# Input projections of a hybrid decoder block in seven quarter products, in two passes over the tokens

## The chip, the cores and the metric

The kernel runs on one core of a Trainium2 chip. Its time is the device time of one execution in microseconds (us). The core has engines that run side by side, each through its own list of instructions in order: PE (matmuls; PEld is its loading of weights), DVE and POOL (elementwise work), ACT (functions and copies), and SP, which issues the DMAs. POOL can't read PSUM, the memory into which PE writes. The order on each engine is fixed when the program is built: a planner places every instruction by the order of the source and by its own estimate of when its operands are there. At run time an instruction that is not ready holds up everything behind it on its engine.

## What is computed

A decoder block over 2048 tokens of width 1024, all in float32:

```python
xn = rmsnorm(h, pre_gain[i])
z = xn @ w_in[i]
q, k, v, fl, g_attn, x_lru, g_lru = jnp.split(z, SPLIT_POINTS, axis=-1)
...
y_attn = rmsnorm(o_attn, attn_out_gain[i]) * jax.nn.silu(g_attn)
xc = causal_depthwise_conv(x_lru, conv_w[i], conv_b[i])
o_lru = rg_lru(xc, ...)
y_lru = rmsnorm(o_lru, lru_out_gain[i]) * jax.nn.silu(g_lru)
mix = jnp.concatenate([y_attn, y_lru], axis=-1) @ w_out[i]
h = h + rmsnorm(mix, post_gain[i])
...
```

`w_in` has 6152 columns: six groups of 1024 (queries, keys, values, gate of the attention, input and gate of the recurrence) and 8 forget logits. `o_attn` is causal attention of 8 heads of 128 whose scores get a bias from the cumulated forget logits; `o_lru` a gated linear recurrence over the tokens. A second matmul with a gate and per-layer embeddings follows; the change doesn't touch it.

## The kernel before

Every float32 operand of a matmul is split in two parts, a high one (ACT copies it to the type that PE reads, line 46) and a low one, the difference (DVE or POOL, line 52). `mm3` then makes three matmuls of a product: high-high, high-low, low-high (lines 60 to 62).

**Projections.** All tokens of `x`, times the gain of the norm, lie in SBUF in both parts (`xh`, `xl`: four chunks of 512 tokens, lines 230 to 234). Beside it the sum of squares of every token is made (line 244), and its root is applied to the results (`rx`, `rs_x`), so matmuls don't wait for it. Values come first: four groups of 256 columns, tokens on partitions, the last group with the forget logits as well (264 columns, `project_v`). Then for each of 8 blocks of 128 features (loop at line 342): the input of the recurrence with its convolution, its gate, the keys, then the recurrence itself (lines 385 to 421), and queries and attention gate of the block before. `load_w` loads a block of weights (two loads of 512 columns' worth) and splits it, with POOL making the lows; `project` makes 24 matmuls of 128x512 for each chunk of 512 tokens: 8 pieces of the contraction times 3. Keys, queries, values and gates go to DRAM as float32 (`kT_d`, `qT_d`, `v_d`, `gT_d`).

**Attention.** 8 heads times 4 groups of 512 queries. While one group's scores are made, the values of the group before are (`merge`). `scores` takes 512 keys at a time; DVE adds the bias and keeps the row's extreme (line 553), ACT makes the exponential (560). `values` transposes the weights on PE (582), splits them (`th` on ACT, `tl` on DVE) and multiplies them with the values. The inverse of the row sums makes a round trip through DRAM (`r_d` out at line 565, `rb` back at 567) and is applied at line 594. The next head's keys and values come in eight pieces during the head before (`load_part`): each is loaded into a buffer `kvf` (two of them), copied by ACT into `kh` or `vh` (line 451 or 455) and completed by POOL (`kl`, `vl`); queries likewise (`split_q`), with the low on DVE. POOL also adds the causal mask to pieces of bias that come by DMA (`dg`, lines 490 and 491). The first head's pieces and queries are loaded beside the last projections (lines 499 to 504). In the last head the weights of the output projection are loaded through `kvf` too.

The order of the blocks and `tc.high_priority` at two places are by hand; the rest is the planner's. A tile's pool has a number of buffers (`bufs`); a new tile waits until its buffer is free.

## Time and profile before

| | us |
|---|---|
| median of three runs (2438.3 to 2449.4) | 2444.1 |
| the profiled execution, first to last instruction (span) | 2421.5 |
| projections, by PE's timeline | 5.5 to 1139.1 |
| attention, seven heads of eight (1150 to 1730) | 580 |

The span is that of one profiled execution, and its total device time is not on the page; the runs of the table were other executions. An engine's "busy" time counts the instructions that it runs. Matmuls overlap in PE's pipeline, so the time of one is read from how many run in a stretch, not from its own duration. In rows of groups the columns are line, engine, operation, output and inputs, shape and count, then busy us and mean ns of one, then idle time before them with what ended it.

### The profile page before, as it was taken

The page shows a single profiled execution, that of the slowest core. Times are in us where ns is not written, and L with a number is a line of the kernel's source. Part 1 is how long each engine was busy: PE and PEld are TensorE (multiplying, and loading weights), DVE is VectorE, ACT ScalarE, POOL GpSimd, SP SyncE. Part 2 cuts the span into 40 slices and gives each one's busy share as a digit, 9 for nine tenths or more (in the row PEclk, how much of TensorE's full clock was granted, in tenths as well). Part 3 has the DMA queues.
Part 4 walks back from the last instruction along what each step waited for, and adds up shares of the span by engine and source line. Part 5 has one row for each costly group of instructions (what it writes and reads, how often), then busy time and mean ns, then how long its engine had stood idle before and what let it go on. Part 6 is the DMA issues. An engine that isn't in the chain of part 4 may idle for free.

```text
span 2421.5 us, 30623 instructions
## 1 busy us (share of the span) xinstructions
PE 2288.7 (95%) x11297; PEld 1895.9 (78%) x11297; DVE 1208.3 (50%) x2193; ACT 908.0 (37%) x1526; POOL 665.1 (27%) x594
## 2 busy tenths in 40 slices
PE   8999999999999999999778778988789999999999
PEld 8998888888888888887667667766668787788887
DVE  5222764555554646363666666766552413433333
ACT  7311432324241414232545545655452423211111
POOL 0210422324141314131322333233242322322221
PEclk9999999999999999999899889999899999999999
DMA  9411111112121212125555555455443635433332
GB/s 327 131 49 31 63 59 57 63 53 70 46 76 40 76 48 74 44 74 138 157 128 124 115 130 140 124 140 131 113 127 109 226 119 191 130 121 110 113 101 83
DMA packets 190519, 257.50 MB, mean 106 GB/s; under 512 B 31648, under 2 KB 104608, under 8 KB 190368
## 3 DMA queue, kind: packets, MB, share of 16 engines
q1 hardware_dynamic: 190224, 255.49, 35.4%
q8 instruction: 89, 1.46, 0.3%
q14 instruction: 62, 0.51, 0.1%
q10 hardware_dynamic: 144, 0.05, 0.0%
HBM read 179.65 MB, written 75.83 MB: 106 GB/s over the span
## 4 chain that ended last, share of the span: by engine, by line
PE 33%; DMA 11%; DVE 3%; issue 2%; ACT 2%; POOL 1%; SPq 0%; DVEq 0%; ACTq 0%; POOLq 0%
PE bank L60 7%; PE bank L62 7%; PE bank L61 7%; DMA kvf<-kT_d 4%; PE tbank L582 3%; DMA dg<-nb_d 2%; PE obank L60 2%; DMA kvf<-in_w_o_dram 2%; PE obank L61 2%; PE obank L62 2%; DMA kvf<-v_d 1%; DMA r_d<-r 1%; DMA ya_d<-gs 1%; DVE pr L553 1%; PE sbank L62 1%
## 5 line engine op out<-in xcount | busy, mean ns | idle before, releaser
L60 PE MATMUL bank<-xh,wh 128*128 128x512 f32 x1280 | 506.0, 395 | 0.0
L61 PE MATMUL bank<-xl,wh 128*128 128x512 f32 x1280 | 505.9, 395 | 0.0
L62 PE MATMUL bank<-xh,wl 128*128 128x512 f32 x1280 | 505.9, 395 | 0.0
L61 PEld LDWEIGHTS bank<-xl,wh 128*128 128x128 f32 x1280 | 240.5, 188 | 58.1
L62 PEld LDWEIGHTS bank<-xh,wl 128*128 128x128 f32 x1280 | 240.5, 188 | 58.0
L60 PEld LDWEIGHTS bank<-xh,wh 128*128 128x128 f32 x1280 | 240.5, 188 | 57.7
L52 DVE TENSOR_TENSOR tl<-tbank,th 128x512 fp32r<-128x512 f32 (+1 forms) x320 | 191.0, 607 | 165.9 <-ACT th L46 164.5
L582 PE MATMUL tbank<-ident,pr 128*128 128x128 f32 x1088 | 182.3, 285 | 43.1 <-DVE tl L52 42.0
L46 ACT ACTIVATE th<-tbank 128x512 fp32r<-128x512 f32 (+1 forms) x320 | 164.3, 527 | 93.5 <-PE tbank L582 89.3
L582 PEld LDWEIGHTS tbank<-ident,pr 128*128 128x128 f32 x1088 | 138.7, 147 | 75.3 <-DVE tl L52 44.8
L60 PE MATMUL obank<-th,vh 128*128 128x512 f32 (+1 forms) x320 | 129.4, 404 | 62.5 <-ACT th L46 58.5
L491 POOL TENSOR_TENSOR dg<-dg,cmask 128x128 f32<-128x128 f32 x128 | 60.8, 478 | 424.5 <-DMA dg<-nb_d 313.8
L52 POOL TENSOR_TENSOR wl<-wf,wh 128x512 fp32r<-128x512 f32 x70 | 96.0, 1393 | 265.1 <-ACT wh L46 265.1
L560 ACT ACTIVATE pr<-pr,m 128x128 f32<-128x128 f32 (+15 forms) x128 | 153.1, 1197 | 11.5 <-DVE m L553 11.5
L60 PE MATMUL bank<-wvh,xh 128*128 128x256 f32 (+1 forms) x512 | 144.2, 285 | 7.2 <-ACT wvh L46 7.2
L52 POOL TENSOR_TENSOR yo<-yf,yh 128x1024 fp32r<-128x1024 f32 x32 | 76.9, 2403 | 254.1 <-ACT yh L46 245.0
L62 PE MATMUL bank<-wvh,xl 128*128 128x256 f32 (+1 forms) x512 | 144.7, 284 | 0.0
L61 PE MATMUL bank<-wvl,xh 128*128 128x256 f32 (+1 forms) x512 | 144.3, 283 | 0.0
L61 PE MATMUL obank<-tl,vh 128*128 128x512 f32 (+1 forms) x320 | 138.4, 432 | 1.1 <-DVE tl L52 1.1
L60 PE MATMUL sbank<-kh,qh 128*128 128x512 f32 (+3 forms) x320 | 127.6, 399 | 9.8 <-DVE m L553 8.8
L60 PEld LDWEIGHTS obank<-th,vh 128*128 128x128 f32 x320 | 64.3, 201 | 85.6 <-ACT th L46 69.1
L61 PE MATMUL sbank<-kl,qh 128*128 128x512 f32 (+3 forms) x320 | 121.4, 379 | 0.0
(214 smaller groups left out, 4668.8 us busy)
## 6 DMA issues: line engine op xcount, KB each, us to landing
wf<-in_w_t_dram SPq DMA_DIRECT2D x80, 256.0 KB, 2.9
xr<-in_x_dram SPq DMA_DIRECT2D x16, 512.0 KB, 6.6
v_d<-vo SPq DMA_DIRECT2D x64, 128.0 KB, 2.1
kT_d<-st SPq DMA_DIRECT2D x32, 256.0 KB, 2.1
yl_d<-G SPq DMA_DIRECT2D x32, 256.0 KB, 2.1
qT_d<-st SPq DMA_DIRECT2D x32, 256.0 KB, 2.1
gT_d<-st SPq DMA_DIRECT2D x32, 256.0 KB, 2.2
dg<-nb_d SPq DMA_DIRECT2D x32, 256.0 KB, 5.7
```

Source lines behind the costliest of these rows:

```text
L46: nc.scalar.activation(hi, src, AF.Copy)
L52: eng.tensor_tensor(out=lo, in0=src, in1=f32(hi), op=ALU.subtract)
L60: nc.tensor.matmul(out, lhsT=wh, rhs=xh, start=start, stop=False)
L61: nc.tensor.matmul(out, lhsT=wh, rhs=xl, start=False, stop=False)
L62: nc.tensor.matmul(out, lhsT=wl, rhs=xh, start=False, stop=stop)
L491: nc.gpsimd.tensor_tensor(out=dg[:, n - P:n], in0=dg[:, n - P:n], in1=cmask, op=ALU.add)
L553: nc.vector.tensor_tensor_reduce(out=pr[:, a:z], in0=b[:, :z - a], in1=dg if z == L else u.bias[:, a:z], scale=-1.0, scalar=BIG if m is No ...
L560: nc.scalar.activation(pr[:, :L], pr[:, :L], AF.Exp, bias=m, scale=-1.0, accum_out=r4[:, i:i + 1])
L582: nc.tensor.transpose(b[:, i * P:(i + 1) * P], u.P[i][:, sb * P:(sb + 1) * P], ident)
```

## The change

The projections are grouped into products of two halves by two halves: the contraction (1024) in two halves, two blocks of features, and two chunks of 512 tokens. Instead of the eight products of quarters, seven products of sums of quarters are made, with Strassen's and Winograd's formulas. `operands` makes the seven sums of the weights: six loads of 512 columns, four sums on DVE, seven splits on ACT and POOL. `x_sums` makes those of `x`. `combine` runs the seven products (`by_feature`: 12 matmuls of 512 columns each; `by_token` for values: 24 of 256), adds later products onto banks of earlier ones where the formula allows it, and makes the remaining sums on DVE (five for each combination, with two copies on ACT).

The seven operands of `x` for 1024 tokens fill the room of the old `xh` and `xl`, so the tokens go in two passes. Weights are loaded and split in each pass. The operands of the second pass are made during the first (`x_sums(2, ...)`, in four of its blocks), written to `bx_d` and read back between the passes. `x` is scaled by its root mean square before the split (`stats`, `x_piece`), so results need no scaling any more. The forget logits get matmuls of their own (`project_forget`). In a pass, each block makes the recurrence's input and gate as one combination, keys and queries as one, and every second block the gates of two heads as one.

Keys, queries and values are stored as high and low part (`two_parts`), and attention loads both parts straight into the operands' tiles; `kvf`, its copies and its differences go for them. The first head's loads stand behind the projections. The queries' factor moves into the constant of the instruction at line 553 and that of the bias. The recurrence keeps its formulas, with its temporary tiles in one set of six buffers.

```diff
-    kT_d = dram.tile([NH, P, S], F32, name="kT_d")
+    kT_d = dram.tile([2, NH, P, S], F32, name="kT_d")
...
+    ORDER = (1, 6, 5, 7, 2, 3, 4)
...
+    def parts(src, el, hi=None, lo=None):
+        if hi is None:
+            hi = wk.tile([P, 512], F32R, name="wh", bufs=NWH)
+            lo = wk.tile([P, 512], F32R, name="wl", bufs=NWH)
+        split(nc, src, hi, lo, "act", el)
+        return hi, lo
+    def operands(load, nq):
+        def raw(r, q):
+            t = wk.tile([P, 512], F32, name="wf", bufs=NWF)
+            src = load(r, q)
+            nc.sync.dma_start(out=t.rearrange("p (a b) -> p a b", b=src.shape[-1]), in_=src)
+            return t
+        def tt(out, a, b, op):
+            nc.vector.tensor_tensor(out=out, in0=a, in1=b, op=op)
+            return out
+        qs = range(nq)
+        yield 1, [parts(raw(11, q), "pool") for q in qs]
+        s1, s2, s3 = [], [], []
+        for q in qs:
+            a21, a22, a11 = raw(21, q), raw(22, q), raw(11, q)
+            s1.append(tt(a22, a21, a22, ALU.add))
+            s3.append(tt(a21, a11, a21, ALU.subtract))
+            s2.append(tt(a11, s1[q], a11, ALU.subtract))
+        yield 6, [parts(s2[q], "pool") for q in qs]
+        yield 5, [parts(s1[q], "pool") for q in qs]
+        yield 7, [parts(s3[q], "pool") for q in qs]
+        a12 = [raw(12, q) for q in qs]
+        yield 2, [parts(a12[q], "pool") for q in qs]
+        yield 3, [parts(tt(s2[q], a12[q], s2[q], ALU.subtract), "pool") for q in qs]
+        yield 4, [parts(raw(22, q), "pool") for q in qs]
+    def combine(load, nq, units, product, sinks):
+        B = [{} for _ in units]
+        for num, ws in operands(load, nq):
+            for n, u in enumerate(units):
+                t = B[n]
+                if num in (1, 5, 6, 7):
+                    t[num] = bank()
+                    product(t[num], num, ws, u, True)
+                else:
+                    product(t[{2: 1, 3: 5, 4: 7}[num]], num, ws, u, False)
+                if num == 1 or num == 5:
+                    t["p", num] = ev()
+                    nc.scalar.activation(t["p", num], t[num], AF.Copy)
+                elif num == 6:
+                    t["u"] = t["p", 1]
+                    nc.vector.tensor_tensor(out=t["u"], in0=t[6], in1=t["p", 1], op=ALU.add)
+                elif num == 7:
+                    t["v"] = t["p", 5]
+                    nc.vector.tensor_tensor(out=t["p", 5], in0=t["p", 5], in1=t["u"], op=ALU.add)
+                    c22, done = sinks(u, 22)
+                    nc.vector.tensor_tensor(out=c22, in0=t[7], in1=t["p", 5], op=ALU.add)
+                    done(c22)
+                elif num == 2:
+                    sinks(u, 11)(t[1])
+                else:
+                    c, done = sinks(u, 12 if num == 3 else 21)
+                    nc.vector.tensor_tensor(out=c, in0=t[5 if num == 3 else 7], in1=t["u"], op=ALU.add)
+                    done(c)
+    bs_ = {}
...
+    def by_feature(out, num, ws, u, start):
+        (wh, wl), = ws
+        wh, wl = (w.rearrange("p (k f) -> p k f", f=P) for w in (wh, wl))
+        bh, bl = bs_[num]
+        for k in range(4):
+            for n, (w, x_) in enumerate(((wh, bh), (wh, bl), (wl, bh))):
+                nc.tensor.matmul(out, lhsT=w[:, k], rhs=x_[:, k], start=start and k == 0 and n == 0,
+                                 stop=k == 3 and n == 2, skip_group_check=True)
+    def by_token(out, num, ws, u, start):
+        bh, bl = bs_[num]
+        for i in range(2):
+            ts = slice((2 * u + i) * P, (2 * u + i + 1) * P)
+            for k in range(4):
+                wh, wl = (w.rearrange("p (k f) -> p k f", f=256)[:, k % 2] for w in ws[k // 2])
+                for n, (x_, w) in enumerate(((bh, wh), (bh, wl), (bl, wh))):
+                    nc.tensor.matmul(out[:, i * 256:(i + 1) * 256], lhsT=x_[:, k, ts], rhs=w,
+                                     start=start and i == 0 and k == 0 and n == 0,
+                                     stop=i == 1 and k == 3 and n == 2, skip_group_check=True)
+    def halves(i1, i2):
+        return lambda r, q: w_t[i1 if r < 20 else i2, :, (r % 10 - 1) * 4:(r % 10) * 4]
+    def two_parts(src, store, el="pool"):
+        hi, lo = evr("sh"), evr("sl")
+        split(nc, src, hi, lo, "act", el)
+        for i, part in enumerate((hi, lo)):
+            store(i, f32(part))
...
+    def stats(t0, pool):
+        ss = wk.tile([P, 8], F32, name="ss", bufs=2)
+        for i in range(4):
+            for j in range(2):
+                xr = pool.tile([P, 512], F32, name="xt")
+                nc.sync.dma_start(out=xr, in_=x[(t0 + i) * P:(t0 + i + 1) * P, j * 512:(j + 1) * 512])
+                nc.scalar.activation(xr, xr, AF.Square, accum_out=ss[:, j * 4 + i:j * 4 + i + 1])
+        s4 = wk.tile([P, 4], F32, name="s4", bufs=2)
+        nc.vector.tensor_tensor(out=s4, in0=ss[:, 0:4], in1=ss[:, 4:8], op=ALU.add)
+        rsqrt_small(rs_x[:, t0:t0 + 4], s4, wk, 4)
+        b = bank()
+        for i in range(4):
+            dg = pool.tile([P, P], F32, name="dg0", bufs=2)
+            nc.vector.tensor_scalar(dg, ident, rs_x[:, t0 + i:t0 + i + 1], None, ALU.mult)
+            nc.tensor.matmul(b[:, i * P:(i + 1) * P], lhsT=onesq, rhs=dg, start=True, stop=True)
+        rx = pool.tile([P, 512], F32, name="rx", bufs=2)
+        nc.scalar.activation(rx, b, AF.Copy)
+        return rx
...
+    def x_piece(c, k, rx, pool):
+        t = pool.tile([P, 512], F32, name="xt")
+        nc.sync.dma_start(out=t, in_=xT[c, :, k])
+        nc.vector.scalar_tensor_tensor(out=t, in0=t, scalar=vec[:, PRE + k:PRE + k + 1], in1=rx,
+                                       op0=ALU.mult, op1=ALU.mult)
+        return t
+    def x_sums(c, k, rxs, pool):
+        def sub(out, a, b):
+            nc.vector.tensor_tensor(out=out, in0=a, in1=b, op=ALU.subtract)
+            return out
+        b11 = x_piece(c, k, rxs[0], pool)
+        yield 1, b11
+        b12 = x_piece(c + 1, k, rxs[1], pool)
+        t1 = sub(b11, b12, b11)
+        yield 5, t1
+        b22 = x_piece(c + 1, k + 4, rxs[1], pool)
+        yield 7, sub(b12, b22, b12)
+        yield 3, b22
+        t2 = sub(b22, b22, t1)
+        yield 6, t2
+        b21 = x_piece(c, k + 4, rxs[0], pool)
+        yield 2, b21
+        yield 4, sub(b21, b21, t2)
...
+    def project_forget(p):
+        lhs = []
+        for j in range(2):
+            w = wk.tile([P, 4, P], F32R, name="wff", tag="wh", bufs=NWH)
+            nc.gpsimd.memset(f32(w), 0.0)
+            f = wk.tile([P, 4, 8], F32, name="wf8", bufs=2)
+            nc.sync.dma_start(out=f, in_=w_f[:, 4 * j:4 * j + 4])
+            split(nc, f, w[:, :, 0:8], w[:, :, 8:16], "act", "dve")
+            lhs.append(w)
+        for i, use in enumerate((((1, 0), (2, 1)), ((1, 0), (5, 0), (3, 1)))):
+            b = bank()
+            n, last = 0, len(use) * 8 - 1
+            for num, j in use:
+                for k in range(4):
+                    for part in bs_[num]:
+                        nc.tensor.matmul(b, lhsT=lhs[j][:, k], rhs=part[:, k], start=n == 0, stop=n == last)
+                        n += 1
+            z = ev()
+            nc.vector.tensor_copy(z[:16], b[:16])
+            nc.sync.dma_start(out=zf_d[:, (2 * p + i) * 512:(2 * p + i + 1) * 512], in_=z[:16])
...
+    def project_kq(p, hb):
+        def sinks(u, c):
+            dst = qT_d if c > 20 else kT_d
+            cs = slice((2 * p + c % 10 - 1) * 512, (2 * p + c % 10) * 512)
+            def store(i, part):
+                nc.sync.dma_start(out=dst[i, hb, :, cs], in_=part)
+            if c == 11:
+                return lambda b: two_parts(b, store, "dve")
+            return ev(), lambda z: two_parts(z, store)
+        combine(halves(5 * hb + 2, 5 * hb + 3), 1, range(1), by_feature, sinks)
...
+            pe = pool_(p0, "pe", NXT0, side="right")
+            rxs = [stats(0, pe), stats(4, pe)]
+            gens = [x_sums(0, k, rxs, pe) for k in range(4)]
+            for i in range(1, 8):
+                bs_[i] = new_b(i)
+            for _ in range(7):
+                for k in range(4):
+                    i, t = next(gens[k])
+                    parts(t, "dve", bs_[i][0][:, k], bs_[i][1][:, k])
...
+                if i == 1 and p == 0:
+                    nc.vector.tensor_copy(halo[:, hb], X[:, 512:515])
+            def gate(i):
+                sg = lt()
+                nc.scalar.activation(sg, Gs[i], AF.Sigmoid)
+                nc.vector.tensor_tensor(out=Gs[i], in0=Gs[i], in1=sg, op=ALU.mult)
+            def sinks(u, c):
+                i = c % 10 - 1
+                if c == 11:
+                    def take(b):
+                        nc.scalar.activation(Xs[0][:, 3:], b, AF.Copy)
+                        conv(0)
+                    return take
+                if c == 12:
+                    return Xs[1][:, 3:], lambda z: conv(1)
+                return Gs[i], lambda z: gate(i)
+            combine(halves(5 * hb, 5 * hb + 1), 1, range(1), by_feature, sinks)
+            for i in range(2):
+                XC, G = XCs[i], Gs[i]
+                XH, XL = lt(F32R, "XH"), lt(F32R, "XL")
+                split(nc, XC, XH, XL, "act", "pool")
+                R, I, Dn = lt(), lt(), lt()
+                for gi, (dst, bias) in enumerate(((R, BR), (I, BI))):
+                    b = bank()
+                    mm3(nc, b, (wgh[:, gi], wgl[:, gi]), (XH, XL), True, True)
+                    nc.scalar.activation(dst, b, AF.Sigmoid, bias=vec[:, bias + hb:bias + hb + 1])
...
+        for p in range(2):
+            if p == 1:
+                for i in ORDER:
+                    bs_[i] = new_b(i)
+                    for n in range(2):
+                        nc.sync.dma_start(out=f32(bs_[i][n]), in_=bx_d[i - 1, n])
+            project_forget(p)
+            for j in range(2):
+                project_v(p, j)
+            if p == 0:
+                rxs = [stats(8, xq), stats(12, xq)]
+            else:
+                xq_stack.close()
+                forget(pool_(pl_, "cw"))
+            for hb in range(NH):
+                recurrent(p, hb)
+                project_kq(p, hb)
+                if hb % 2:
+                    project_ga(p, hb - 1)
+                if p == 0 and 1 <= hb < 5:
+                    k = hb - 1
+                    for i, t in x_sums(2, k, rxs, xq):
+                        for n, part in enumerate(parts(t, "pool")):
+                            nc.sync.dma_start(out=bx_d[i - 1, n, :, k], in_=f32(part))
+            sl = wk.tile([P, 8], F32, name="sl", bufs=1)
+            channel_sums(sl, accl, 0, 8, bank)
+            rsqrt_small(rstd_l[:, 8 * p:8 * p + 8], sl, wk, 8)
+    p1.close()
+    ps1.close()
...
-        f = ap.tile([P, 4, P], F32, name="kvf", bufs=2) if h else wp.tile([P, 4, P], F32, name="wf")
-        if n % 2 == 0:
-            cs = slice(c * 512, (c + 1) * 512)
-            f = f.rearrange("p a b -> p (a b)")
-            nc.sync.dma_start(out=f, in_=kT_d[h, :, cs])
-            split(nc, f, s.kh[:, cs], s.kl[:, cs], "act", "pool" if h else "dve")
-        else:
-            bs = slice(c * 4, c * 4 + 4)
-            nc.sync.dma_start(out=f, in_=v_d[h, :, bs])
-            split(nc, f, s.vh[:, bs], s.vl[:, bs], "act", "pool" if h else "dve")
...
+        for i in range(2):
+            if n % 2 == 0:
+                nc.sync.dma_start(out=f32((s.kh, s.kl)[i][:, cs]), in_=kT_d[i, h, :, cs])
+            else:
+                nc.sync.dma_start(out=f32((s.vh, s.vl)[i][:, bs]), in_=v_d[i, h, :, bs])
...
-        u.qh, u.ql = early_q.pop(g) if h == 0 and g in early_q else split_q(h, g)
+        for i, q in enumerate((u.qh, u.ql)):
+            nc.sync.dma_start(out=f32(q), in_=qT_d[i, h, :, g * 512:(g + 1) * 512])
...
-                                               scale=-1.0, scalar=BIG if m is None else m,
+                                               scale=-QSCALE, scalar=BIG if m is None else m,
```

403 lines of the change are left out of this document (126 added, 277 removed).

## The prediction

> **What bounds the kernel now.** I read the page's totals first, then busy time by stretches, then PE's timeline at the seams, and last who waited for whom inside attention.
>
> ```profile
> span 2421.5 us, 30623 instructions
> PE 2288.7 (95%) x11297; PEld 1895.9 (78%) x11297; DVE 1208.3 (50%) x2193; ACT 908.0 (37%) x1526; POOL 665.1 (27%) x594
> ...
> 0.00:30.00 30.00, 22.85 (x168) 22.30 (x169) 20.09 (x47) 23.08 (x43) 2.74 (x13) 1.00 0.97 345
> 5.40:1139.10 1133.70, 1131.95 (x5625) 948.77 (x5626) 565.40 (x810) 381.95 (x565) 293.43 (x221) 1.00 0.23 78
> 120.00:180.00 60.00, 60.00 (x509) 60.00 (x508) 12.14 (x56) 9.97 (x21) 12.67 (x5) 1.00 0.18 49
> 500.00:600.00 100.00, 100.00 (x431) 80.64 (x430) 49.76 (x65) 30.48 (x42) 27.44 (x21) 1.00 0.17 55
> 1150.00:1730.00 580.00, 488.17 (x2646) 406.83 (x2646) 389.10 (x967) 322.65 (x598) 182.34 (x223) 0.91 0.53 130
> ...
> 1139.14 0.22 PE L60 MATMUL sbank<-kh,qh 128*128 128x128 f32 x1
> ...
> L46 ACT ACTIVATE kh<-kvf 128x512 fp32r<-128x512 f32 x28 | 17.7, 631 | 121.5 <-DMA kvf<-kT_d 120.7 <-POOL dg L491 0.8
> ```
>
> The rows of stretches give window, length, busy time of PE, PEld, DVE, ACT and POOL, PE's clock, the DMA share and GB/s. The projections last until 1139 us (the last row but one, the first score). From 5.4 us on PE never stops in them: 431 matmuls of 512 columns in 100 us are **0.232 us** each, 509 of 256 columns (V) in 60 us are **0.118 us**. DVE is half busy there, POOL a quarter. Attention is another matter: PE is idle for 92 of 580 us and its granted clock is 0.91. Those 580 us hold the loads of 28 pieces of keys (last row), four a head, so seven heads, and a head takes 83 us. The runs shown have a median of 2444.1, 22.6 over this span; I take these 22.6 as unchanged, so that a difference in the span is a difference in the time.
>
> **The change, part by part.**
>
> *Matmuls.* A pair of feature blocks over all tokens needs 2 x 4 x 24 = 192 matmuls now; two passes of seven products of 12 need 168. Twenty pairs: 3360 for 3840, so 480 x 0.232 = 111 us less. V: 1344 for 1536, 192 x 0.118 = 23 us less. The forget logits leave V's last group (8 of 264 columns, 1 us) and become 80 matmuls of their own, 19 us more. PE's work falls by about **116 us**. The Trainium skill, TensorE: Matmul & The Clock Gate, section "Back-to-back issue gap", gives about 131 ns for each 512-column matmul in a stream; at that figure the 480 would be worth 63 us, but the 0.232 above was measured in this kernel, and it decides.
>
> *What the seven products ask of the other engines.* Take one cycle: two head blocks in one pass, with two recurrent, two key/query and one gate combination.
>
> ```profile
> L402 DVE RECIPROCAL Dn<-Dn 128x512 f32<-128x512 f32 x32 | 107.3, 3354 | 1.1
> L406 DVE TENSOR_TENSOR X<-X,Dn 128x512 f32<-128x512 f32 x32 | 22.5, 704 | 0.4
> L409 DVE TENSOR_TENSOR_SCAN R<-Dn,carry,I 128x512 f32<-128x512 f32 x24 | 31.7, 1323 | 1.0
> L233 DVE SCALAR_TENSOR_TENSOR xl<-xf,vec,xh 128x512 fp32r<-128x512 f32 x24 | 16.6, 747 | 4.7 <-ACT xh L232 4.7
> L408 DVE TENSOR_SCALAR Dn<-Dn 128x512 f32<-128x512 f32 x20 | 8.4, 419 | 0.0
> L420 POOL TENSOR_TENSOR R<-R 128x512 f32<-128x512 f32 x28 | 29.2, 1041 | 64.0 <-DVE G L413 64.0
> L46 ACT ACTIVATE wh<-wf 128x512 fp32r<-128x512 f32 x80 | 46.2, 623 | 100.3 <-PE bank L61 93.6 <-DMA wf<-in_w_t_dram 6.7
> ...
> 694.71 1.29 POOL L52 TENSOR_TENSOR wl<-wf,wh 128x512 fp32r<-128x512 f32 x1 [1.26 <-ACT wh L46]
> 695.96 1.74 POOL L52 TENSOR_TENSOR wl<-wf,wh 128x512 fp32r<-128x512 f32 x1
> ...
> 695.32 0.63 DVE L334 SCALAR_TENSOR_TENSOR st<-bank,rx 128x512 f32<-128x512 f32 x1
> 695.87 0.69 DVE L406 TENSOR_TENSOR X<-X,Dn 128x512 f32<-128x512 f32 x1
> 696.66 1.60 DVE L407 TENSOR_TENSOR I<-I,X 128x512 f32<-128x512 f32 x1
> ```
>
> PE: 5 x 84 + 24 for the gates = 444 matmuls, **103 us**. DVE: each combination makes 4 sums of weights and 5 sums of results (45), the two recurrent blocks 12 more two-tensor operations, the key/query lows 2: 59 x 0.69 = 41. 20 of the scalar-and-two-tensors kind x 0.75 = 15, 8 x 0.42, 4 reciprocals x 3.35 = 13, 4 scans x 1.3 = 5, small copies 1: **79 us**. POOL: 35 lows of weights, 6 of results, 12 in the recurrence: 53 x 1.29 + 4 x 1.04 + two small ones = **75 us**. ACT: 35 + 10 + 12 copies of 0.62 and the recurrence's functions, some 67 us, which stays beside PE. So each by itself fits under PE's 103.
>
> But DVE and POOL are not by themselves. In the last five rows POOL's second `wl` starts at 695.96 while DVE's L406 runs, and takes 1.74 where the first took 1.29; DVE's L407 starts within it, and ends at 698.26, 0.56 after POOL's end: 1.60 where L406, of the same form, took 0.69. Each **waited for the other to finish**. L334, which reads PSUM and one tile of SBUF, ran beside POOL in 0.63: such operations don't take part. Where now 27 of 100 us are POOL's, meetings are rare; after the change POOL fills 75 of 103. The Trainium skill, GPSIMD Engine Reference, section "Specifications", says that POOL's SBUF interfaces are shared with VectorE and names contention with instructions of two SBUF inputs or in a 2-port mode; it gives no price, and the 1.60 agrees.
>
> The price of a meeting lies between 0 (as L334) and 0.91 (1.60 - 0.69). In a cycle 68 DVE operations have two SBUF inputs or are of the fast 0.42 kind (5 for each combination, 25 in all; convolution 12; gates, tail of the recurrence and silu 31). Half of them follow another one directly (three in a convolution, five in the recurrence's tail, three sums of weights); POOL takes its turn between those, so they pay 0.91, and the first of a run about half. With POOL busy for 0.72 of the time: 0.72 x (34 x 0.91 + 34 x 0.45) = 33 us. DVE then needs 79 + 33 = **112 us a cycle**, over PE's 103: the projections go at DVE's pace. Ends: 103 (no cost, PE rules) and 79 + 0.72 x 68 x 0.91 = 123.
>
> *Eight cycles.* 896 us. In pass 0 four blocks also make the sums of the later tokens: 4 x (4 x 0.75 + 4 x 0.69 + 8 x 0.72 x 0.68) = 39 us of DVE. So pass 0 takes 487, pass 1 448.
>
> *Start.* Now the first matmul runs at 5.5 us and PE loses 7 us in the first 30 (row above). Afterwards x is scaled by its rms, so 4.2 MB of statistics come before it: 12 us at the 345 GB/s of that row, and squares, root and broadcast bring the first piece to about 18 us. DVE then owes 16 pieces x 0.75 + 16 differences x 0.69 + 28 lows x 0.69 = 42 us; the last operand is ready at 60. Until then PE can run four products of V's first group (192 x 0.118 = 23) and the forget logits (9): 28 us idle. V and logits of a pass are 672 x 0.118 + 9 = 89 us, so this part ends at 117.
>
> *Seam of the passes.* 14.7 MB of operands come back, 43 us at 345 GB/s, each pair as soon as its last product is done; the rest of the last combination (17 us) and V's products (5.7 us each against 6.1 us of loading) cover all but some 5 us. Bounds: nothing, and 43 - 17 = 26. I take 5.
>
> *End of the projections.*
>
> ```profile
> rb<-r_d SPq DMA_DIRECT2D x32, 256.0 KB, 4.4
> ...
> kvf<-kT_d SPq DMA_DIRECT2D x28, 256.0 KB, 4.7
> ```
>
> The first head's keys and queries came in beside the last projections; now their tiles take the place of the recurrence's and are loaded after it. No row shows it; two loads of 4.7 us one after the other (the last number is the median from issue to landing) make 9, and 0 is the other end; I take 8, as nothing else is ready then.
>
> Projections: 117 + 487 + 5 + 89 + 448 + 8 = **1154**, against 1139: +15.
>
> *Attention.* Splitting of keys, values and queries goes.
>
> ```profile
> 1241.23 0.46 POOL L491 TENSOR_TENSOR dg<-dg,cmask 128x128 f32<-128x128 f32 x1 [13.82 <-DMA dg<-nb_d]
> ...
> 1242.09 1.23 SPq L565 DMA_DIRECT2D r_d<-r  x1
> ...
> 1253.20 0.32 SPq L567 DMA_DIRECT2D rb<-r_d  x1
> ...
> 1249.60 0.63 ACT L46 ACTIVATE kh<-kvf 128x512 fp32r<-128x512 f32 x1 [11.94 <-DMA kvf<-kT_d]
> ...
> 1250.74 0.69 DVE L52 TENSOR_TENSOR tl<-tbank,th 128x512 fp32r<-128x512 f32 x1 [10.05 <-ACT th L46]
> ...
> 1251.49 1.11 PE L582 MATMUL tbank<-ident,pr 128*128 128x128 f32 x4 [8.59 <-DVE tl L52]
> ...
> PE obank L60 <- ACT th L46: 58.5, 23, 14.9
> PE tbank L582 <- DVE tl L52: 42.0, 11, 9.4
> ...
>   DMA kvf<-kT_d: 120.7, 27
>   DMA kvf<-v_d: 40.8, 16
> ```
>
> Read upwards from PE: it stood 8.59 us for DVE's `tl`, which stood 10.05 for ACT's `th`, which was queued behind `kh`, which stood 11.94 for the load of the **next** head's keys; that load needed a buffer that POOL frees, and POOL stood 13.82 for a bias. ACT lost 162 us so. With the parts loaded straight into their tiles, a head ahead, nothing of this is left on ACT or POOL (POOL's lows moved to the projections, and are in the 75 above). What PE loses now is 92 us idle and 0.09 x 580 = 52 at the lowered clock; the gain lies between 0 and 144. Next in line is the round trip of 1/sum: `r_d` goes out at 1242.09, SP can issue `rb` only at 1253.20, and it lands 4.4 us later, 15 us in all. After a head's first group PE has only some 8 us of work (128 x 10 columns of values and 128 x 26 of scores, three matmuls each, and transposes), so about 7 us a head come back as a wait of DVE. Loads also grow, by 12 x 256 KB a head. I take half of the 144, 10 us a head: **-70** over seven heads; the eighth, which splits weights of the output, stays.
>
> **Sum**: 2444 + 15 - 70 = **2389**.
>
> **The rivals.**
> *A. PE stays the bound.* Meetings cost DVE nothing that PE sees: the order lets them fall into DVE's spare 24 us. Cycles of 103, and the sums of later tokens hide: 117 + 412 + 5 + 89 + 412 + 8 = 1043, -96; with -70, 2278. For it: the 100% of PE today; against: POOL and DVE together exceed a cycle.
> *B. Slower: every meeting costs its full 0.91.* Cycles of 123, late sums 45: 117 + 537 + 5 + 89 + 492 + 8 = 1248, +109; with -70, 2483. The cycle decides: over about 121 us the kernel is slower by more than 0.5%.
> *C. Attention gives nothing back*, since `rb`, the biases and the larger loads (DMA share 0.53 today) take the place of `kvf`: 2444 + 15 - 5 = 2454.
>
> **How the numbers follow.** Chances: forecast 0.48 (its own range 2335 to 2435, from cycles of 107 to 117 us), A 0.24, B 0.18, C 0.10. A difference of 0.5%, 12 us, is about what a measurement of this kernel can tell from no change. Faster by more: nearly all of the forecast and A, 0.68. Within it: the edge of the forecast and half of C, 0.12. Slower: B, half of C, 0.20. The range leaves out half of A's lower side and what lies beyond B: 2280 to 2485.
>
> **What would show it.** The step of the matmuls: some 670 fewer by count less 80, and 0.232 us unchanged. The cycle: in the middle of a pass a PE busy share near 0.92, DVE over 0.95 with waits inside its operations, mean time of L406's form near 1.1 instead of 0.70. Attention: no wait for `kvf`, a head in about 73 us, a wait of `on` for `rb`, a clock near 0.97. The start: PE sparse until 60 us. I am wrong if PE is full in the passes (A), or if a head still takes 80 us (C).

## The result and the profile after

The change made the kernel slower. Four executions took 2651.4 to 2665.0 us, median **2656.1**; the kernel before took 2441.2 on the same chip. The ratio is 1.089 with an interval of 1.085 to 1.093. The forecast was 2389 with a range of 2280 to 2485.

The page of the changed kernel begins so (span, then busy time of each engine with its share of the span and its instructions):

```profile
span 2663.2 us, 32138 instructions
...
PE 2251.5 (85%) x10704; PEld 1842.9 (69%) x10704; DVE 1565.4 (59%) x2446; ACT 1099.5 (41%) x1882; POOL 1134.5 (43%) x916
```

593 matmuls are gone, as counted, but PE is busy for 85% of the span where it was for 95%. The span grew by 242 us. Read by stretches of the changed kernel (window, length, busy time with instructions of PE, PEld, DVE, ACT and POOL, PE's clock, DMA share, GB/s):

```profile
0.00:60.00 60.00, 24.91 (x118) 21.14 (x118) 47.44 (x98) 34.07 (x71) 18.08 (x22) 0.95 0.52 178
200.00:680.00 480.00, 375.50 (x1460) 291.67 (x1459) 352.84 (x381) 219.86 (x348) 310.65 (x222) 0.86 0.42 138
900.00:1260.00 360.00, 305.53 (x1221) 239.19 (x1219) 267.97 (x281) 170.86 (x266) 226.15 (x161) 0.89 0.34 112
1393.00:1973.00 580.00, 480.26 (x2654) 403.23 (x2654) 367.86 (x937) 282.68 (x513) 109.20 (x166) 0.92 0.73 168
...
1382.96 0.45 PE L66 MATMUL sbank<-kh,qh 128*128 128x128 f32 x1 [19.52 <-DMA qh<-qT_d]
```

The second and third row lie inside pass 0 and pass 1. PE, full before, stands for 104 of 480 and 54 of 360 us there, and its clock is 0.86 and 0.89. DVE is busy for 74% of both, so it isn't full either. The fourth row is seven heads of attention: 580 us, as before. The last row is the first score: the projections end at 1383.0 where they ended at 1139.1. So **all of the loss, 244 us, lies in the projections**, and attention (first score to last value matmul) took 698.0 where it took 695.2. (These are two single profiles. By the medians on the same chip the loss is 215 us, some 30 less: this profile ran 7 us over its kernel's median, that of before some 20 under it.)

By PE's first and last matmul of each phase, in us, beside the forecast's terms; the last two columns are two of the experiments below:

| phase | forecast | after | e5_both | e12_best_after |
|---|---|---|---|---|
| statistics, V and logits of pass 0 | 117 | 150 | 140 | 142 |
| eight blocks of pass 0 | 487 | 568 | 491 | 506 |
| seam, V and logits of pass 1 | 94 | 119 | 94 | 93 |
| eight blocks of pass 1 | 448 | 525 | 464 | 451 |
| end, to the first score | 8 | 21 | 21 | 22 |
| projections | 1154 | 1383 | 1211 | 1214 |

What PE waited for in the passes of the changed kernel (us in total, times, longest):

```profile
PE bank L66 <- ACT XH L52: 133.0, 30, 6.8
PE bank L257 <- ACT wh L52: 33.5, 4, 10.9
PE bank L67 <- POOL XL L58: 17.4, 15, 1.9
PE bank L268 <- POOL wl L58: 13.9, 2, 12.5
```

The largest wait is that of the recurrence's gates for `XH`, the split output of the convolution: 30 times, 133 us. One such place in the timeline of the changed kernel (start, duration, engine, line, operation; in brackets how long the engine stood and for what), ACT's rows, then one of DVE, then PE's:

```profile
994.26 0.61 ACT L52 ACTIVATE XH<-XC 128x512 fp32r<-128x512 f32 x1
997.81 0.69 ACT L476 ACTIVATE lt<-bank,vec 128x512 f32<-128x512 f32 x1 [2.93 <-PE bank L68]
...
1000.03 1.28 ACT L481 ACT_TABLE_LOAD   x1
1001.33 0.72 ACT L481 ACTIVATE lt<-lt,tiny 128x512 f32<-128x512 f32 x1
1001.96 0.61 ACT L52 ACTIVATE XH<-XC 128x512 fp32r<-128x512 f32 x1
...
995.29 1.75 DVE L445 SCALAR_TENSOR_TENSOR XC<-X,vec,XC 128x512 f32<-128x512 f32 x1
...
994.93 0.73 PE L66 MATMUL bank<-XH,wgh 128*128 128x512 f32 x2 [2.90 <-ACT XH L52]
996.55 0.79 PE L67 MATMUL bank<-XL,wgh 128*128 128x512 f32 x1 [0.89 <-POOL XL L58]
997.14 0.63 PE L68 MATMUL bank<-XH,wgl 128*128 128x512 f32 x1
...
998.00 0.63 PE L68 MATMUL bank<-XH,wgl 128*128 128x512 f32 x1
1002.62 1.22 PE L66 MATMUL bank<-XH,wgh 128*128 128x512 f32 x2 [4.00 <-ACT XH L52]
1003.64 0.63 PE L257 MATMUL bank<-bh,wh 128*128 128x512 f32 x1
1004.07 0.63 PE L257 MATMUL bank<-bl,wh 128*128 128x512 f32 x1
...
1006.20 0.63 PE L257 MATMUL bank<-bh,wh 128*128 128x512 f32 x1
1006.63 0.47 PE L257 MATMUL bank<-bl,wh 128*128 128x512 f32 x1
```

The gates of the first half wait 2.90 us for `XH`. Their result goes to ACT, whose functions for that half (and a load of its tables) come before the second half's `XH` on ACT's list: it ends at 1002.57, and PE, whose list has the second half's gates next, has stood 4.00 us. The operands of the next product were there, but behind the gates on the list. Then a second cost shows: matmuls of 512 columns start some 0.43 us apart until 1006.6, where they take 0.233 otherwise. The slow spell had begun before the second stand: the three from 997.14 to 998.00 are 0.43 apart too. It came with the stands of 2.90 and 0.89 us, went on through that of 4.00, and ended after 4 us of matmuls. The Trainium skill, TensorE: Matmul & The Clock Gate, section "What's actually happening", says that PE falls to half clock after an idle window of about 3.4 us and is released after a busy one of that length. These rows agree with the release; the fall came here after 2.90 us, two matmuls and 0.89 us, none of these stands as long as that window.

In attention of the changed kernel, by the same kind of list:

```profile
DVE on L693 <- DMA rb<-r_d: 77.6, 11, 12.5
ACT pr L659 <- DMA r_d<-r: 71.1, 7, 12.1
PE obank L66 <- DVE on L693: 62.0, 10, 11.0
PE sbank L66 <- DMA qh<-qT_d: 54.3, 13, 19.5
...
SPq L666 <- DMA r_d<-r: 193.4, 27, 11.6
```

The waits for `kvf` of keys and values are gone, as the prediction said. In their place stands the round trip of the softmax's 1/sum: `on` waits for `rb`, PE's next group for `on`, the exponential for the buffer of the sums, and SP's list, with the next queries behind it, stands 193 us at `rb`.

### The profile page after: what moved, and what is told of

It is laid out like the page before. It is cut to its first block, busy times and chain, and to the rows that moved or that the text cites. A ratio compares the mean times of both kernels' runs of the same rounds, so it can differ in the third digit from the quotient of the medians.

```text
span 2663.2 us, 32138 instructions
## 1 busy us (share of the span) xinstructions
PE 2251.5 (85%) x10704; PEld 1842.9 (69%) x10704; DVE 1565.4 (59%) x2446; ACT 1099.5 (41%) x1882; POOL 1134.5 (43%) x916
## 4 chain that ended last, share of the span: by engine, by line
PE 48%; DMA 15%; DVE 3%; POOL 2%; issue 2%; ACT 2%; SPq 1%; DVEq 0%; POOLq 0%; ACTq 0%
PE bank L257 14%; PE bank L67 7%; PE bank L66 7%; PE bank L68 7%; DMA r_d<-r 3%; PE tbank L681 3%; DMA ya_d<-gs 2%; DMA rb<-r_d 2%; PE obank L66 2%; PE obank L68 2%; PE obank L67 2%; DMA qh<-qT_d 1%; DMA ql<-qT_d 1%; DMA kvf<-in_w_o_dram 1%; PE sbank L66 1%
## 5 line engine op out<-in xcount | busy, mean ns | idle before, releaser
L58 POOL TENSOR_TENSOR wl<-wf,wh 128x512 fp32r<-128x512 f32 x336 | 487.5, 1465 | 254.9 <-ACT wh L52 228.9
L257 PE MATMUL bank<-bh,wh 128*128 128x512 f32 x1120 | 457.9, 409 | 33.5 <-ACT wh L52 33.5
L257 PE MATMUL bank<-bl,wh 128*128 128x512 f32 x1120 | 456.0, 407 | 0.0
L257 PE MATMUL bank<-bh,wl 128*128 128x512 f32 x1120 | 449.5, 403 | 0.0
L52 ACT ACTIVATE wh<-wf 128x512 fp32r<-128x512 f32 x336 | 205.1, 623 | 251.3 <-PE bank L257 156.8
L257 PEld LDWEIGHTS bank<-bh,wh 128*128 128x128 f32 x1120 | 221.3, 198 | 88.7 <-ACT wh L52 35.3
L195 DVE TENSOR_TENSOR wf<-wf 128x512 f32<-128x512 f32 x192 | 200.8, 1046 | 136.1 <-DMA wf<-in_w_t_dram 44.3
L257 PEld LDWEIGHTS bank<-bl,wh 128*128 128x128 f32 x1120 | 220.3, 197 | 53.1
L257 PEld LDWEIGHTS bank<-bh,wl 128*128 128x128 f32 x1120 | 217.7, 194 | 53.1 <-POOL wl L58 0.6
L268 PE MATMUL bank<-wl,bh 128*128 128x256 f32 x448 | 130.2, 293 | 18.4 <-POOL wl L58 18.3
```

The source lines that it names most:

```text
L52: nc.scalar.activation(hi, src, AF.Copy)
L58: eng.tensor_tensor(out=lo, in0=src, in1=f32(hi), op=ALU.subtract)
L195: nc.vector.tensor_tensor(out=out, in0=a, in1=b, op=op)
L257: nc.tensor.matmul(out, lhsT=w[:, k], rhs=x_[:, k], start=start and k == 0 and n == 0, stop=k == 3 and n == 2, skip_group_check=True)
L268: nc.tensor.matmul(out[:, i * 256:(i + 1) * 256], lhsT=x_[:, k, ts], rhs=w, start=start and i == 0 and k == 0 and n == 0, stop=i == 1 and ...
```

## The experiments

For the projections there are two theories. **Q**, the queue (called list theory later): the place of the gates on PE's fixed list costs the time; whatever the other engines do, PE stands until a chain of convolution, ACT and gates is through. **P**, the port: operations of DVE with two inputs in SBUF and those of POOL shut each other out, so every chain through DVE is stretched. The changed kernel's 336 lows of weights on POOL are what it added there. For attention: the round trip took the place of the splits (rival C of the prediction), or the larger loads did. In the rounds of the experiments the kernel before took 2413 to 2421 us, not 2441, so they are compared by their phases rather than by their totals.

**1. Gates later.** The gates, and all of the recurrence behind them, are moved behind the key/query combination.

```diff
             combine(halves(5 * hb, 5 * hb + 1), 1, range(1), by_feature, sinks)
+            yield
             for i in range(2):
...
-                recurrent(p, hb)
+                rec = recurrent(p, hb)
+                next(rec)
                 project_kq(p, hb)
+                next(rec, None)
```

> The changed kernel, with the gates' matmuls and the rest of the recurrence put behind the key/query combination of the same block. Theory Q (PE's fixed order: the matmuls of the gates stand among the products and hold PE until XH is there, 133 us in 30 waits within the passes, each followed by a lowered clock): the wait for XH falls below 40 us, the clock in the passes rises from 0.88 to over 0.95, the projections end before 1260 us instead of 1383, the whole below 2540 us. Theory P (the forecast's: DVE, held up by POOL at their common port, sets the pace): the wait only moves to other matmuls, the projections still end after 1330 us, the whole over 2600 us.

Measured: 2577.1 us; projections 1310, 73 less. The passes of this kernel, in the same kind of list:

```profile
PE bank L66 <- ACT XH L52: 106.9, 16, 12.6
PE bank L257 <- ACT wh L52: 20.4, 2, 10.3
```

Only half as many waits are left (the first half of a block finds its `XH` ready), but the second half's is longer, for it still stands behind the first half's functions on ACT. So the place counts, but neither theory got its whole.

**2. No lows of weights on POOL.** ACT makes a copy of the whole in their place, so they are not lower parts any more and the results differ.

```diff
-        split(nc, src, hi, lo, "act", el)
+        if el == "pool":
+            nc.scalar.activation(hi, src, AF.Copy)
+            nc.scalar.activation(lo, src, AF.Copy)
+        else:
+            split(nc, src, hi, lo, "act", el)
```

> The changed kernel, with the low parts of the weights and of the later tokens' sums made by ACT as a copy of the value instead of by POOL as a difference (336 + 28 operations of 1.3 us leave POOL and the port; the results differ). Theory P: DVE's sums of weights fall from 1.05 to about 0.70 us each, and with the meetings gone the projections end before 1250 us. Theory Q: DVE gets faster just as much, but the wait of PE for XH stays above 90 us, since between the first half's gates and the second half's XH stand ACT's functions; the projections end after 1300 us.

Measured: 2543.6 us; projections 1289, 94 less. DVE's sums of weights, 1046 ns on average in the changed kernel, took 745:

```profile
L199 DVE TENSOR_TENSOR wf<-wf 128x512 f32<-128x512 f32 x192 | 142.9, 745 | 110.4 <-DMA wf<-in_w_v_dram 37.3 <-DMA wf<-in_w_t_dram 31.1 <-ACT wl L185 28.1
```

PE still waited 103 us for `XH` in 30 waits, as Q said, and yet the time fell by more than Q allowed. Both theories hold in part.

**3. More buffers.** Eight tiles in place of six for the recurrence's temporaries (three in place of five for the pieces of `x`).

```diff
-NLT = 6
+NLT = 8
-NXT = 5
+NXT = 3
```

> The changed kernel with eight instead of six buffers for the recurrence's temporary tiles (and three instead of five for the pieces of the later tokens). If the six buffers are what makes the second half's XH wait until the first half's functions are done, half of the waits for XH go (133 to about 70 us) and the projections shorten by 60 to 120 us. If the order on PE and ACT alone does it, or DVE's pace, nothing changes by more than 30 us.

Measured: 2651.7 us; projections 1401, the wait for `XH` 132.5. Buffers of the recurrence are not the cause. (Attention came out at 666 us here with an unchanged program; in the six runs with the changed kernel's attention it lies between 666 and 698, so differences of 30 us between single profiles of it say nothing.)

**4. Parts alone.** The projections of before, with keys, queries and values split there, stored in parts, and loaded straight into the operands' tiles. In short:

```diff
-    kT_d = dram.tile([NH, P, S], F32, name="kT_d")
+    kT_d = dram.tile([2, NH, P, S], F32, name="kT_d")
...
+        split(nc, st, hl[0], hl[1], "act", "pool")
+        for i in range(2):
+            nc.sync.dma_start(out=dst[i, hb, :, c * 512:(c + 1) * 512], in_=f32(hl[i]))
...
+        for i in range(2):
+            if n % 2 == 0:
+                nc.sync.dma_start(out=f32((s.kh, s.kl)[i][:, cs]), in_=kT_d[i, h, :, cs])
```

> The kernel before with its old projections, but keys, queries and values stored as parts and loaded straight into place (the later half of the change alone; of the first head only the first queries are loaded early). The forecast's step: attention falls by about 70 us, from 695 to 625, and the whole to 2370. The rival (the loads of twice the bytes and the round trip of 1/sum take the place of the waits for the splitting, as the changed kernel's 698 us suggest): attention stays within 20 us of 695, the whole between 2430 and 2465; the projections stay at 1139 us in both, since PE is full there.

Measured: 2447.7 us, ratio to before 1.010 (1.008 to 1.013). Projections 1171, 32 more than before, and attention 692: the parts bring it next to nothing. In its attention:

```profile
DVE on L598 <- DMA rb<-r_d: 71.5, 8, 14.0
ACT pr L564 <- DMA r_d<-r: 61.2, 6, 13.7
PE obank L60 <- DVE on L598: 55.6, 7, 12.5
```

These are the waits of the changed kernel, without a Strassen product near. So attention's missing gain has nothing to do with the products.

**5. Both 1 and 2.**

> Both edits of the first two runs in one: the gates and the rest of the recurrence stand behind the key/query combination, and the lower parts of the weights are made by ScalarE instead of GpSimd (they then aren't the true lower parts). Alone the two took 73 and 94 us off the projections (1383 to 1310 and 1289 us). If place and port are two causes, they add up: projections 1190 to 1240 us, total about 2470. If both shorten the same wait (the chain of the convolution up to XH), the second brings little: projections 1260 to 1300, total about 2530.

Measured: 2471.0 us; projections 1211, 172 less than after. Apart the two gave 73 and 94, 167 in sum: **they add up**, so the place of the gates and the lows on POOL are two causes. The passes of this kernel:

```profile
200.00:620.00 420.00, 369.93 (x1513) 295.83 (x1512) 287.61 (x389) 302.92 (x510) 109.40 (x84) 0.94 0.50 164
780.00:1180.00 400.00, 368.86 (x1529) 295.84 (x1528) 277.09 (x347) 277.06 (x457) 112.76 (x84) 0.96 0.36 121
```

The clock came back with the shorter waits: 0.94 and 0.96 where it was 0.86 and 0.89.

**6. Gates that don't wait.** They multiply by a block of `x` that stands ready, so they come out as other numbers; `XH` and `XL` are still made.

```diff
-                    mm3(nc, b, (wgh[:, gi], wgl[:, gi]), (XH, XL), True, True)
+                    mm3(nc, b, (wgh[:, gi], wgl[:, gi]), (bs_[1][0][:, 0], bs_[1][1][:, 0]), True, True)
```

> The changed kernel; the gates' matmuls multiply by a block of the normalized input that stands ready, not by XH and XL, which are still made. Every matmul, function and load is there; only TensorE's wait for the convolution's chain is gone (the gates come out as other numbers). If that wait sets the pace (list theory): its 133 + 17 us go and part of the lowered clock with them, projections 1190 to 1250 us, clock in the passes 0.93 or more. If VectorE with the shared port sets it (port theory): the waits turn up at the banks of the products or at the weights' parts, projections above 1320. In between: each has a share.

Measured: 2576.8 us; projections 1316. With 150 us of waits taken out, 67 were gained. PE's waits in this kernel's passes:

```profile
PE bank L257 <- ACT wh L52: 58.0, 5, 19.0
PE bank L257 <- DVE ev L236: 53.8, 17, 5.4
PE bank L257 <- ACT ev L228: 36.1, 19, 5.3
```

Behind the wait for `XH` stood the next ones: for the sums of products on DVE, which free a bank (`ev` of line 236), and for ACT's copies. So the place is not all, which fits the gain of run 2, which left the gates where they were. How much of these waits is stretching and how much DVE's plain load, this run doesn't show.

**7. No round trip of 1/sum.** No `r_d`, no `rb`: each output is multiplied by ones, and the division by the sums is left out.

```diff
+    rb1 = av.tile([P, 512], F32, name="rb1", bufs=1)
+    nc.gpsimd.memset(rb1, 1.0)
...
-        nc.sync.dma_start(out=r_d[rr].rearrange("(q p) -> p q", p=P), in_=r4)
-        u.rb = av.tile([P, 512], F32, name="rb")
-        nc.sync.dma_start(out=u.rb, in_=r_d[rr:rr + 1, :].broadcast_to([P, 512]))
+        u.rb = rb1
```

> The changed kernel without the trip of the reciprocals of the softmax's sums through DRAM: no r_d store, no rb load, each output is multiplied by a tile of ones (the division by the sums is left out). If the trip is what took over from the split's waits: attention (first score to last value matmul) 600 to 650 us instead of 698, and the waits for qh fall under 25 us, because SP's queue no longer stands at rb. If the loads of keys, queries and values set the time: 665 to 700, the waits for qh stay at 40 or more.

Measured: 2507.9 us; attention **540** in place of 698, more than any theory had given. Most of its attention, as a stretch:

```profile
1390.00:1850.00 460.00, 456.75 (x2694) 393.59 (x2693) 372.85 (x956) 287.41 (x521) 118.36 (x174) 0.99 0.64 205
```

PE is full, its clock is 0.99, and a head takes 63 us where it took 83. The waits for `qh` fell from 54 to 22 us, 19 of them the first queries'. The larger loads (DMA share 0.64) hide.

**8. `rb` issued later.** The loads of `rb` and `gs` are written at the fourth step of the values' loop, to keep SP's list free for the next queries before.

```diff
-        u.rb = av.tile([P, 512], F32, name="rb")
-        nc.sync.dma_start(out=u.rb, in_=r_d[rr:rr + 1, :].broadcast_to([P, 512]))
...
+            if st == 3:
+                rr = h * 4 + g
+                u.rb = av.tile([P, 512], F32, name="rb")
+                nc.sync.dma_start(out=u.rb, in_=r_d[rr:rr + 1, :].broadcast_to([P, 512]))
...
```

> The changed kernel; the loads of rb and gs are issued at the fourth step of the values' loop, not at the end of the scores, so SP's queue stands at rb less and what comes behind it (queries, biases) goes out sooner. If the block of the queue is the cost: waits for qh under 25 us, attention 640 to 675. If the trip itself is: attention 680 to 720, and the waits at rb grow.

Measured: 2641.0 us; attention 675, inside the spread named at run 3; `on` still waited 63 us for `rb`, and PE 45 for `qh`. SP's own waits tell why:

```profile
SPq L675 <- DMA r_d<-r: 178.3, 24, 10.1
```

SP stood 178 us at `rb`, where it stood 193: the edit hardly freed its list, and neither case of the expectation came out whole. So this run doesn't tell the block of SP's list from the length of the trip. Run 7 took both away, and which of them costs how much stays open.

**9 to 11. The sums through TensorE.** The same answer without DRAM: DVE puts high and low part of the reciprocals on diagonals, PE adds them over a tile of ones, ACT copies the bank to `rb`. Nothing is left out. Run 9 is the kernel before with this edit, run 10 the changed kernel, run 11 the kernel of run 4.

```diff
-        nc.sync.dma_start(out=r_d[rr].rearrange("(q p) -> p q", p=P), in_=r4)
...
-        nc.sync.dma_start(out=u.rb, in_=r_d[rr:rr + 1, :].broadcast_to([P, 512]))
...
+        nc.vector.tensor_copy(rh, r4)
+        nc.vector.tensor_tensor(out=rl, in0=r4, in1=f32(rh), op=ALU.subtract)
...
+        for i in range(4):
+            for d_, r_ in ((u.dh, f32(rh)), (u.dl, rl)):
+                nc.vector.tensor_scalar(d_[:, i * P:(i + 1) * P], ident, r_[:, i:i + 1], None, ALU.mult)
...
+            if st == 2:
+                b = psT.tile([P, 512], F32, name="tbank")
+                nc.tensor.matmul(b, lhsT=ones_r, rhs=u.dh, start=True, stop=False)
+                nc.tensor.matmul(b, lhsT=ones_r, rhs=u.dl, start=False, stop=True)
+                u.rb = av.tile([P, 512], F32, name="rb", bufs=1)
+                nc.scalar.activation(u.rb, b, AF.Copy)
```

> The kernel before; the reciprocals of the softmax's sums don't go through DRAM: VectorE puts their two parts on diagonals (8 operations of 128x128 a stage), TensorE adds them up over a tile of ones (two matmuls of 512 columns), ScalarE copies the bank to rb. Nothing is left out. If the trip through DRAM with SP's queue behind it is what bounds the attention of before too (its waits for kvf then being only what stands behind rb in the queue): attention 560 to 610 us instead of 695, total 2280 to 2330. If the splits of keys, queries and values bound it by themselves (the prediction's reading): attention above 640, total above 2360.

> The changed kernel with the same edit (sums' reciprocals through TensorE, nothing left out). The run without the trip had an attention of 540 us; the edit costs TensorE 32 x 2 x 0.232 = 15 us and VectorE some 50 us of 540: attention 550 to 580, total about 2525. Against the kernel before with the same edit it tells what storing in parts is worth once the trip is gone: by the prediction's step some 70 us of attention; by the rival nothing, then both attentions agree within 10 us.

> The projections of before with keys, queries and values stored in parts (the fourth run) and the sums' reciprocals through TensorE. Projections 1171 as in the fourth run; attention as in the changed kernel with the edit, 550 to 580; total about 2310. It is faster than before with the edit alone if storing in parts is worth more than its 32 us in the projections, slower if not.

Measured, with the ratio to the kernel before (2416.4 in these rounds):

| | us | ratio | projections | attention |
|---|---|---|---|---|
| e9_before_pe | 2350.6 | 0.972 (0.970 to 0.974) | 1139 | 623 |
| e10_after_pe | 2538.6 | 1.050 (1.048 to 1.052) | 1381 | 571 |
| e11_parts_pe | 2335.4 | 0.966 (0.963 to 0.968) | 1172 | 580 |

A stretch of attention of run 9, and one of run 10:

```profile
1145.00:1680.00 535.00, 488.75 (x2713) 401.38 (x2714) 476.51 (x1261) 342.80 (x629) 188.86 (x230) 0.98 0.45 133
```

```profile
1393.00:1870.00 477.00, 465.53 (x2699) 396.45 (x2700) 416.98 (x1216) 295.74 (x539) 112.64 (x170) 0.99 0.62 192
```

So there are four attentions: splits and trip 695, parts and trip 692 (run 4) or 698 (after), splits without the trip 623, parts without it 580 or 571. **The trip hides the splits.** Take away the splits alone and little or nothing is won (by the spread of run 3, at most some 30 us in the changed kernel), since the trip still holds things up; take away the trip alone, 72 us; both, 115 to 124. With the trip gone, parts are worth 43 to 52 us, some 9 a head (75 in run 9, 66 in run 10); PE is busy for 0.91 of the stretch in run 9 and for 0.98 in run 10. Run 9 came out between the two cases of its expectation: the splits are a bound of their own, but a lower one than the trip. The attentions of runs 10 and 11 lie in their ranges; run 11's total came out 25 us over the expected one.

**12. The best of the change.** Gates later, the lows of weights on DVE in place of POOL (true lows), the sums through TensorE.

```diff
-        split(nc, src, hi, lo, "act", el)
+        split(nc, src, hi, lo, "act", "dve" if el == "pool" else el)
```

> The changed kernel with the gates and the rest of the recurrence behind the key/query combination, the weights' lower parts made by VectorE instead of GpSimd (true lower parts, nothing left out), and the sums' reciprocals through TensorE. If the meetings at the shared port were GpSimd's doing, VectorE's own operations get shorter by about what it takes over (7 x 0.69 us a combination): projections 1200 to 1260, total 2340 to 2400. If VectorE's load sets the pace: projections 1290 or more, total above 2430.

Measured: 2377.9 us, ratio 0.983 (0.980 to 0.986); projections 1214, attention 568. The groups that share the port, of the changed kernel, and then of run 12 (line, engine, operation, tiles, shape, count, busy us, mean ns, idle before):

```profile
L195 DVE TENSOR_TENSOR wf<-wf 128x512 f32<-128x512 f32 x192 | 200.8, 1046 | 136.1 <-DMA wf<-in_w_t_dram 44.3 <-DMA wf<-in_w_v_dram 27.9 <-POOL wl L58 22.2
L445 DVE SCALAR_TENSOR_TENSOR XC<-X,vec,XC 128x512 f32<-128x512 f32 x96 | 100.5, 1060 | 0.1
L58 POOL TENSOR_TENSOR wl<-wf,wh 128x512 fp32r<-128x512 f32 x336 | 487.5, 1465 | 254.9 <-ACT wh L52 228.9 <-PE bank L257 9.5 <-issue 9.3
```

```profile
L195 DVE TENSOR_TENSOR wf<-wf 128x512 f32<-128x512 f32 x192 | 151.4, 790 | 38.1 <-DMA wf<-in_w_v_dram 18.8 <-DMA wf<-in_w_t_dram 18.5 <-DVE wf L195 0.2
L445 DVE SCALAR_TENSOR_TENSOR XC<-X,vec,XC 128x512 f32<-128x512 f32 x96 | 85.2, 905 | 2.3 <-ACT XC L442 2.2
L58 DVE TENSOR_TENSOR wl<-wf,wh 128x512 fp32r<-128x512 f32 x336 | 251.9, 759 | 33.8 <-ACT wh L52 30.9 <-ACT lt L478 1.9
...
200.00:620.00 420.00, 362.28 (x1481) 287.59 (x1480) 387.81 (x524) 223.13 (x352) 114.49 (x78) 0.93 0.49 157
780.00:1180.00 400.00, 373.12 (x1561) 298.96 (x1560) 372.37 (x478) 223.24 (x348) 125.87 (x87) 0.97 0.38 126
```

DVE took over 336 operations, 252 us of work, and yet the projections became 169 us shorter than those of the changed kernel, 96 shorter than with the gates alone moved (run 1, 1310), with DVE now busy for 92 and 93% of the passes: so DVE's load by itself did not set the pace of the changed kernel. What POOL did in 1465 ns DVE does in 759, and DVE's own sums and convolution come down from 1046 and 1060 ns to 790 and 905. Whether it is the meetings themselves or POOL's slower lows that cost the most was not taken apart; PE's direct waits for `wl` in the passes of after, 13.9 us above, speak for the meetings.

Run 11 is the fastest of all: the projections of before, parts, and the sums through TensorE. It beats run 12 by its projections, 1172 to 1214. Even with its two causes mended, the change's 116 us less of matmuls don't come through.

## Why the prediction was wrong

The forecast of the span was 55 under that of before, the result is 242 over it: 297 us apart, 229 of them in the projections, 73 in attention, 5 less in the rest. (The medians lie 267 apart, as this profiled execution ran 7 over its median where that of before ran 23 under; so up to 30 of the 297 may be the two profiles'.)

- **The matmuls: right.** 593 fewer; 0.233 us each where PE doesn't wait.
- **The cycle: here it failed (158 of the 229).** The step was "DVE then needs 112 us a cycle, over PE's 103: the projections go at DVE's pace". A pass has four cycles; measured are 142 us in pass 0 (forecast 122) and 131 in pass 1 (112). Not DVE's pace: DVE was busy 268 of 360 us, 97 of a cycle's 131, under the 112. The price of meetings was rather too high: the four sums of weights of a combination take 1046 ns on average, 0.36 over 0.69, where the step's shares give 0.72 x (2 x 0.45 + 2 x 0.91) / 4 = 0.49. What it left out is order. It added up each engine's work and took the largest; but gates stand on PE's list right behind a chain DVE, ACT, PE, ACT, and PE can't go round them. A pass 1 cycle is 103 us of matmuls, 20 of standing (54 of 360), and a rest of 8 at a granted clock of 0.89. Runs 1 and 2 gave 73 and 94 us and both together 172: a chain at a bad place, and lows on POOL that stretch DVE's operations. With both mended, a cycle took 116 us (run 5) and 113 (run 12) in pass 1. There, in run 12, both PE and DVE are busy for 93%, so which of them sets the pace is not shown.
- **Start, seam and end: mis-sized, 71 together.** 117 for the start was 150: PE was busy for 25 of the first 60 us, not 32, and made some 118 matmuls in them, where the sum counted 192 for V and 40 for the logits. The rest of V then ran almost dense, and after it PE stood for the statistics of the later tokens (`stats`, line 299), a term that the sum left out; the first product of the blocks starts at 150.40:

```profile
60.00:140.00 80.00, 76.95 (x614) 76.37 (x614) 41.32 (x54) 38.23 (x83) 50.20 (x39) 0.95 0.77 230
...
148.42 1.22 PE L299 MATMUL bank<-dg,onesq 128*128 128x128 f32 x4 [8.18 <-DVE dg L298]
```

The seam with V was 119, not 94; it was 95 in run 2, where the lows left POOL, 94 and 93 in runs 5 and 12, and 112 with the gates alone moved (run 1), so there it was mostly POOL's lows. The end was 21, not 8: one wait of 19.5 us for the first queries. Runs 2, 5 and 12 took some 10 off the start; the rest of it and the end were read from the trace.
- **Attention: the gain was real, the next in line was mis-sized.** "About 7 us a head come back as a wait" for the trip of 1/sum. Without the trip a head takes 63 us, with it 83: in the changed kernel the trip costs about 20 a head, not 7. By this profile that eats the gain whole; in the five other kernels with the same attention (runs 1, 2, 3, 5, 6) it took 666 to 679 us, 16 to 29 under before. With the trip gone the parts bring 43 to 52 us, some 9 a head. That this is near the term of 10 is luck: the term was a half of what PE lost, taken with the trip still there.
- **The rivals.** C, attention gives nothing back, came nearest: nothing by this profile, 16 to 29 of the 70 by the five others. B had the right sign by the wrong means: the cycle did pass its 121, but at 74% of DVE.

## What to carry to other kernels

A sum of busy times by engine is a lower bound; before taking work off a full engine, walk its list and ask what each instruction there waits for, through which engines, and what stands behind it. Where a wait goes, price the next one in line by taking it out as well: a wait can be worth next to nothing until another is gone, as the splits were (3 us with the trip there, 43 to 52 without). A small transfer through DRAM and back was the other one here. A chain that leaves the chip's engines for a broadcast of 512 numbers can be had from TensorE with a diagonal and ones.

## What the runs showed that was not expected

The trip of 2 KB through DRAM cost 158 of 698 us (126 to 158 by the spread of run 3): in the changed kernel's attention the store in pieces of 4 bytes took 11.0 us to land (median), the load of 256 KB behind it 4.9 (rows of its DMA view: queue, count, KB each, median us to landing):

```profile
rb<-r_d SPq DMA_DIRECT2D x32, 256.0 KB, 4.9
...
r_d<-r SPq DMA_DIRECT2D x32, 2.0 KB, 11.0
```

Whether larger pieces would shorten it was not tried. On TensorE the same broadcast is two matmuls of 0.43 us by their own durations; the rows of run 10:

```profile
L685 PE MATMUL tbank<-dh,ones_r 128*128 128x512 f32 x32 | 14.0, 436 | 0.2 <-DVE dh L673 0.2
L686 PE MATMUL tbank<-dl,ones_r 128*128 128x512 f32 x32 | 13.2, 414 | 2.2 <-DVE dl L673 2.2
```

With DVE's diagonals and ACT's copy the broadcast leaves attention at 571 us, against 540 without any division (run 7).

And a row of waits costs PE more than its length: the nine matmuls after the stand of 4.00 us took some 0.44 us each in place of 0.233, some 2 us more. Where waits are many, the granted clock of a stretch (0.86 in pass 0) falls with them and comes back when they go (0.94 in run 5).
